# Expert one-hot codes laid out by pairs of tokens, in operations of eight tokens

## The chip, the core and the metric

The kernel runs on one core of a Trainium2 chip. The metric is the device time of one execution in microseconds; the median of three runs is 1916.95 us (1915.26 to 1919.09). TensorE (PE) multiplies, VectorE (DVE), ScalarE (ACT) and GpSimd (POOL) work element by element, and SyncE (SP) issues most transfers.

## What is computed

The whole kernel is a block of three mixers (windowed attention, a gated recurrence, attention over a memory), an expert layer, a delta-rule layer, a dilated-window attention and two plain feed-forward layers, on 256 tokens of width 1024 in float32. The change lies in the expert layer alone:

```python
idx = jnp.take_along_axis(cand_i, best_pos, axis=-1)
gate = jax.nn.softmax(best_v, axis=-1)
u = u_tab[ix]
act = jax.nn.gelu(jnp.einsum('chkd,cd->chk', u, hx).astype(jnp.float32))
vv = v_tab[ix]
return jnp.einsum('chk,chkd->cd', (gx * act).astype(vv.dtype), vv)
```

Each token picks 8 x 16 = 128 experts of 16384 and weighs each with a gate. An expert's index is a pair: a first key (0 to 127) and a second key (0 to 127).

## The kernel before

The kernel doesn't gather. It multiplies each token with all 16384 rows of `peer_u` (128 chunks of 128 experts, `gemm_y`), keeps the activations as `act` (second key on the partitions, first key and token on the free axes), multiplies `act` with a gate that is zero for the experts a token did not pick, and multiplies the result with all 128 chunks of `peer_v` (`gemm_k`). Each chunk is 24 matmuls: weights and operand are each split into a high and a low part of float32r (`whi` by ACT, `wlo` by DVE or POOL), and three of the four products are added. For `peer_u` POOL makes every second `wlo`; for `peer_v` DVE makes all.

The gates of a token form a 128 x 128 matrix (second key by first key). `scatter` (L1071) builds it from one-hot codes. The 128 picks of a token lie on the partitions; `i1T`, `i2T` hold the first and second key of each pick by token, `g2T` the gate as a high and a low half in float16. For four tokens at a time DVE makes `oh2` (L1080, 128 x 128 x 4: does the second key equal the number in `iota4`), `oh1` (L1083, 128 x 64 x 4, half of the first keys) and `ohg` (L1086, `oh1` times both halves of the gate, 128 x 2 x 64 x 4). PE then adds, for each token, `oh2` (weights, 128 columns) times `ohg` (64 columns moving) for both halves of the gate into the token's 64 columns of a PSUM bank `gp`. Eight tokens fill the bank; DVE then multiplies `act` with it in place (L1094).

All codes lie in one tile, `ohp` (4096 float16 per partition), with the token innermost: `oh2` has three places of 512, `oh1` two of 256, `ohg` three of 512. A matmul takes one token, so PE reads every fourth element. A DVE operation that reuses a place waits for the matmuls that read it.

`scatter(half)` runs for 64 of the first keys over the 256 tokens, 32 rounds of eight tokens. It is a generator with two yields a round (after the codes and matmuls, and after the product with `act`). `bg.step` (class `Bg`) takes as many steps after each chunk as the constants say, so that the code's place in the loop sets the order: `scatter(0)` runs beside `peer_u` chunks from 73 on (1.3 steps a chunk, `UP`), `scatter(1)` beside the first 64 `peer_v` chunks (one step a chunk). [...] Two PSUM banks serve `gp` in turn (`aux`).

Of the kernel before, what the change touches and what calls it, by code (L numbers as in the profile page):

```python
# [15 lines left out]
F16 = mybir.dt.float16  # L16
AF = mybir.ActivationFunctionType
ALU = mybir.AluOpType
# [344 lines left out]
def build(tc, a, out, stop=None, dbg=None):  # L363
    nc = tc.nc
    V, S, PE, G = nc.vector, nc.scalar, nc.tensor, nc.gpsimd
    ctx = ExitStack()
    with ctx:
# [65 lines left out]
        def mm(o, l, r, start, stop):  # L433
            x = PE.matmul(o, l, r, start=start, stop=stop, skip_group_check=True)  # L434
            if dbg is not None:
                dbg.append((st.plan[st.nu - 1][0], x.ins.name))
# [13 lines left out]
        def aux(nm="aux"):  # L450
            return aux_p.tile([128, 512], F32, name=nm, tag="aux")
# [170 lines left out]
        with ExitStack() as pa:  # L622
# [35 lines left out]
            for c in range(4):  # L658
                hi, lo = st.get(("w_vm", c))
                for j in range(2):  # L660
                    kt = c * 2 + j
                    w = slice(j * 512, (j + 1) * 512)
                    for t in range(2):
                        tt = slice(t * 128, (t + 1) * 128)
# [154 lines left out]
            for c in range(2):  # L819
                hi, lo = st.get(("w_va", c))  # L820
                for j in range(4):
                    kt = c * 4 + j
                    w = slice(j * 256, (j + 1) * 256)
                    for t in range(2):
                        o = vps[:, t * 256:(t + 1) * 256]
                        tt = slice(t * 128, (t + 1) * 128)
# [63 lines left out]
            for n in range(8):  # L890
                if n + NG < 8:
                    gts.append(gates(n + NG))
                g = gts.pop(0)
# [48 lines left out]
        with ExitStack() as pb:  # L942
            B1 = pb.enter_context(tc.tile_pool(name="B1", bufs=1))
            bp = pb.enter_context(tc.tile_pool(name="bp", bufs=2))
# [10 lines left out]
            for t in range(2):  # L955
                for g in range(4):
                    p = aux("sc")
# [11 lines left out]
            i1T, i2T = i12T[:, 0, :], i12T[:, 1, :]  # L969
            g2T = bp.tile([128, 2, T], F16, name="g2T", tag="g2T", bufs=1)  # L970
# [3 lines left out]
            iota = bp.tile([128, 128], F32, name="iota", bufs=1)  # L974
# [90 lines left out]
                    V.scalar_tensor_tensor(g2T[:, 1, w], gf, GS, g2T[:, 0, w], op0=ALU.mult, op1=ALU.subtract)  # L1065
                    yield

            iota4 = bp.tile([128, 128, 4], F16, name="iota4", tag="iota4", bufs=1)
            V.tensor_copy(iota4, iota[:, :, None].to_broadcast([128, 128, 4]))

            def scatter(half):  # L1071

                c0 = half * 64
                for t0 in range(0, T, 8):
                    p = aux("gp")
                    for k in (0, 4):
                        tt = slice(t0 + k, t0 + k + 4)
                        i = (t0 + k) // 4
                        oh2 = ohp[:, 512 * (i % 3):512 * (i % 3) + 512].rearrange("p (c t) -> p c t", t=4)
                        V.tensor_tensor(oh2, iota4, i2T[:, None, tt].to_broadcast([128, 128, 4]), op=ALU.is_equal)  # L1080
                        o1 = 1536 + 256 * (i % 2)
                        oh1 = ohp[:, o1:o1 + 256].rearrange("p (c t) -> p c t", t=4)
                        V.tensor_tensor(oh1, iota4[:, c0:c0 + 64, :], i1T[:, None, tt].to_broadcast([128, 64, 4]), op=ALU.is_equal)  # L1083
                        o1 = 2048 + 512 * (i % 3)
                        ohg = ohp[:, o1:o1 + 512].rearrange("p (q c t) -> p q c t", q=2, t=4)
                        V.tensor_tensor(ohg, oh1[:, None, :, :].to_broadcast([128, 2, 64, 4]),  # L1086
                                        g2T[:, :, None, tt].to_broadcast([128, 2, 64, 4]), op=ALU.mult)
                        for j in range(4):
                            for q in range(2):
                                mm(p[:, (k + j) * 64:(k + j + 1) * 64], oh2[:, :, j], ohg[:, q, :, j],  # L1090
                                   k == 0 and j == 0 and q == 0, q == 1)
                    yield
                    av = act[:, c0:c0 + 64, t0:t0 + 8]
                    V.tensor_tensor(av, p.rearrange("p (t c) -> p c t", c=64), av, op=ALU.mult)  # L1094
                    yield
# [7 lines left out]
            bg.drain()  # L1103
            ohp = res.tile([128, 4096], F16, name="ohp", tag="x")
            bg.add(scatter(0))
            for c in range(UP[0], 128):
                ps = gemm_y(("peer_u", c), hb)
                S.activation(act[:, c, :], ps, AF.Gelu_apprx_tanh)
                with tc.issue_after(st.lasts[-LAG]):
                    bg.step(UP[2])  # L1110
            bg.drain()
            bg.add(scatter(1))
            acc = acc_new()
            cq = (opr.tile([128, 8, T], F32R, name="chi", tag="xhi"), opr.tile([128, 8, T], F32R, name="clo", tag="xlo"))
# [26 lines left out]
        with ExitStack() as pc:  # L1141
# [413 lines left out]
            for c, h in gorder:  # L1555
# [9 lines left out]
                elif c == "v":  # L1565
                    vf = cp.tile([128, T], F32, name="vf", tag="vf")
                    conv(ps, 16 + h, vf)
                    p = aux("vT")
# [71 lines left out]
        with ExitStack() as pd:  # L1640
# [26 lines left out]
            for j in range(2):  # L1667
                p = aux("trc")
# [16 lines left out]
            for w in (slice(0, 512), slice(512, 768)):  # L1685
                p = aux("bias")
                p = p[:18, :w.stop - w.start]
# [131 lines left out]
        c = N.sums()  # L1819
# [31 lines left out]
```

## Time and profile before

| what | value |
|---|---|
| median of three runs | 1916.95 us (1915.26 to 1919.09) |
| profiled execution, its own time | 1913.9 us |
| its span in the trace | 1912.1 us |
| granted TensorE clock, mean | 0.984 |
| PE / DVE / ACT / POOL busy | 96% / 72% / 51% / 18% |
| DMA | 314.85 MB, 165 GB/s in the mean |

The span runs from the first to the last instruction in the trace; the 1.8 us between span and time lie around it. Busy shares are means over all stages. Matmuls overlap, so what one costs is read from the distance of the starts, or from a run of them on the chain, rather than from its own duration.

### The profile page before, as it was taken

To read this page: it belongs to the slowest core of one execution; us is meant where nothing else is said; L and a number is where in the kernel's file an instruction comes from. 1 tells how busy PE (TensorE), PEld (TensorE's weight loads), DVE (VectorE), ACT (ScalarE), POOL (GpSimd) and SP (SyncE) were. 2 spreads that over 40 slices of the span, in tenths; PEclk is the share of its full clock that TensorE was granted. 3 is DMA by queue.
4 is the path that set the end of the run, shared out by engine and by line. 5 is a ranking of instruction groups with operands and counts; after the bars stand their busy time and mean duration, and the time that the engine had idled before them with its cause. 6 is when DMAs were issued, how large, how long until landed. Compare 5 with 4: busy or idle time off the path is not lost.

```text
span 1912.1 us, 38492 instructions
## 1 busy us (share of the span) xinstructions
PE 1835.9 (96%) x15622; PEld 1799.8 (94%) x15622; DVE 1375.9 (72%) x2644; ACT 974.2 (51%) x1589; POOL 344.7 (18%) x202
## 2 busy tenths in 40 slices
PE   8999999999999999999999998878999999999998
PEld 7989999999999999999999997767999999999998
DVE  8698666887868777888865558996575556766555
ACT  6587444545443334444354455634755456555554
POOL 2010002344443332000000026553130001010000
PEclk9999999999999999999999998889999999999998
DMA  6534566455654445455566664344156666645663
GB/s 229 181 122 140 181 193 209 149 186 177 189 174 155 149 152 165 158 163 156 160 204 188 188 205 132 93 97 115 47 163 188 189 189 205 191 134 187 189 188 109
DMA packets 113704, 314.85 MB, mean 165 GB/s; under 512 B 35043, under 2 KB 38243, under 8 KB 112759
## 3 DMA queue, kind: packets, MB, share of 16 engines
q1 hardware_dynamic: 112390, 305.82, 52.4%
q0 software_dynamic: 1136, 6.59, 1.0%
q8 instruction: 122, 2.00, 0.4%
q14 instruction: 56, 0.45, 0.1%
HBM read 307.06 MB, written 5.30 MB: 163 GB/s over the span
## 4 chain that ended last, share of the span: by engine, by line
PE 82%; DVE 14%; ACT 2%; issue 2%; DMA 0%; POOL 0%; DVEq 0%; SPq 0%; ACTq 0%
PE mmps L434 37%; PE acc L434 34%; PE gp L434 3%; DVE wlo L206 2%; PE p L434 2%; PE vps L434 1%; DVE cy L1265 1%; DVE tk L1042 1%; DVE U L1303 1%; ACT whi L202 1%; DVE tk L1040 1%; DVE kv L1349 1%; DVE eg L1461 1%; DVE mxl L443 1%; PE lg L434 1%
## 5 line engine op out<-in xcount | busy, mean ns | idle before, releaser
L202 ACT ACTIVATE whi<-wraw 128x1024 fp32r<-128x1024 f32 x562 | 595.7, 1061 | 775.1 <-PE acc L434 296.9
L206 DVE TENSOR_TENSOR wlo<-wraw,whi 128x1024 fp32r<-128x1024 f32 x461 | 569.7, 1237 | 306.0 <-ACT whi L202 303.0
L204 POOL TENSOR_TENSOR wlo<-wraw,whi 128x1024 fp32r<-128x1024 f32 x101 | 247.1, 2449 | 672.1 <-ACT whi L202 577.2
L434 PE MATMUL mmps<-bhi,whi 128*128 128x256 f32 x1024 | 288.9, 282 | 1.9 <-ACT act L1100 1.9
L434 PE MATMUL mmps<-bhi,wlo 128*128 128x256 f32 x1024 | 285.8, 279 | 3.1 <-DVE wlo L206 3.1
L434 PE MATMUL mmps<-blo,whi 128*128 128x256 f32 x1024 | 285.8, 279 | 0.0
L434 PE MATMUL acc<-chi,whi 128*128 128x256 f32 x1008 | 283.4, 282 | 0.0
L434 PE MATMUL acc<-clo,whi 128*128 128x256 f32 x1008 | 281.3, 279 | 0.3 <-DVE clo L441 0.3
L434 PE MATMUL acc<-chi,wlo 128*128 128x256 f32 x1008 | 281.1, 279 | 0.0
L434 PEld LDWEIGHTS mmps<-bhi,wlo 128*128 128x128 f32 x1024 | 192.5, 188 | 3.5 <-DVE wlo L206 3.5
L434 PEld LDWEIGHTS mmps<-bhi,whi 128*128 128x128 f32 x1024 | 193.2, 189 | 2.5 <-ACT act L1100 2.5
L434 PEld LDWEIGHTS mmps<-blo,whi 128*128 128x128 f32 x1024 | 192.6, 188 | 0.0
L434 PEld LDWEIGHTS acc<-clo,whi 128*128 128x128 f32 x1008 | 189.5, 188 | 0.5 <-DVE clo L441 0.5
L434 PEld LDWEIGHTS acc<-chi,whi 128*128 128x128 f32 x1008 | 189.9, 189 | 0.0
L434 PEld LDWEIGHTS acc<-chi,wlo 128*128 128x128 f32 x1008 | 189.4, 188 | 0.0
L434 PE MATMUL acc<-rl,whi 128*128 128x256 f32 x512 | 142.8, 279 | 0.0
L434 PE MATMUL acc<-rh,wlo 128*128 128x256 f32 x512 | 142.8, 279 | 0.0
L434 PE MATMUL acc<-rh,whi 128*128 128x256 f32 x512 | 142.4, 279 | 0.0
L434 PE MATMUL mmps<-mxl,whi 128*128 128x256 f32 x496 | 139.3, 281 | 1.4 <-DVE mxl L443 1.0
L434 PE MATMUL mmps<-mxh,wlo 128*128 128x256 f32 x496 | 138.9, 280 | 0.8 <-DVE wlo L206 0.8
L434 PE MATMUL mmps<-mxh,whi 128*128 128x256 f32 x496 | 138.6, 280 | 0.8 <-ACT mxh L439 0.5
L434 PE MATMUL mmps<-xhi,whi 128*128 128x256 f32 x384 | 111.2, 289 | 1.8 <-DVE qm L862 1.3
(578 smaller groups left out, 4429.3 us busy)
## 6 DMA issues: line engine op xcount, KB each, us to landing
wraw<-in_peer_u SPq DMA_DIRECT2D x128, 512.0 KB, 3.6
wraw<-in_peer_v SPq DMA_DIRECT2D x128, 512.0 KB, 3.8
wraw<-in_w SPq DMA_DIRECT2D x128, 512.0 KB, 4.2
wraw<-in_w_gates SPq DMA_DIRECT2D x24, 512.0 KB, 3.6
wraw<-in_p_all SPq DMA_DIRECT2D x16, 512.0 KB, 3.8
wraw<-in_w_peer_q SPq DMA_DIRECT2D x16, 512.0 KB, 3.8
wraw<-in_d_v SPq DMA_DIRECT2D x12, 512.0 KB, 4.4
wraw<-in_d_q SPq DMA_DIRECT2D x9, 512.0 KB, 4.4
```

The lines of the kernel that those rows point to most:

```text
L202: nc.scalar.activation(hi, t, AF.Copy)
L204: nc.gpsimd.tensor_tensor(lo, t, hi.bitcast(F32), op=ALU.subtract)
L206: self.lasts.append(nc.vector.tensor_sub(lo, t, hi.bitcast(F32)).ins)
L434: x = PE.matmul(o, l, r, start=start, stop=stop, skip_group_check=True)
L443: return V.scalar_tensor_tensor(lo, src, scale, hi.bitcast(F32), op0=ALU.mult, op1=ALU.subtract).ins
L1040: V.tensor_tensor(eq, io16, rank[:, s, None].to_broadcast([128, 32, 16]), op=ALU.is_equal)
L1042: V.tensor_tensor(eq.rearrange("p (h k) c -> p h k c", h=2), eq.rearrange("p (h k) c -> p h k c", h=2), tif4[:, h:h + 2, p2, None, :].to_b ...
L1265: V.scalar_tensor_tensor(y[:, lo_:hi_], x[:, lo_ + d:hi_ + d], col("gdn_conv", j * 24 + base), y[:, lo_:hi_], op0=ALU.mult, op1=ALU.add)
L1303: V.scalar_tensor_tensor(U[:, u, :], kk[:, h, t, :], rk2b[:, t, d, h:h + 1], D[:, u, :], op0=ALU.mult, op1=ALU.mult)
L1349: V.tensor_tensor(q, M[:, 0:i, 0:i].rearrange("p j c -> p c j"), L[:, i, None, 0:i].to_broadcast([128, i, i]), op=ALU.mult)
L1461: (G if QE == "G" else V).tensor_mul(qe[d], qe[d], qf[:, h, (1 - d) * 128:(2 - d) * 128])
```

## The change

The codes are made for eight tokens in one operation. The free axes are now four pairs of tokens, key, and token of the pair, so that the two tokens of a pair lie next to each other and PE reads every second element. `iota4` keeps its size, but only its first half (`iota2`, 128 x 2) is filled and read, repeated over the pairs. `oh2` has two places of 1024, `oh1` one of 512, and the gate product is made in two operations, one for each half of the gate, in three places of 512. The matmuls run over the eight tokens for the high half of the gate, then over the eight tokens for the low half; only the very first still starts the bank.

```diff
--- before.py
+++ after.py
@@ -1065,30 +1065,28 @@
                     V.scalar_tensor_tensor(g2T[:, 1, w], gf, GS, g2T[:, 0, w], op0=ALU.mult, op1=ALU.subtract)
                     yield
 
-            iota4 = bp.tile([128, 128, 4], F16, name="iota4", tag="iota4", bufs=1)
-            V.tensor_copy(iota4, iota[:, :, None].to_broadcast([128, 128, 4]))
+            iota4 = bp.tile([128, 2, 128, 2], F16, name="iota4", tag="iota4", bufs=1)
+            iota2 = iota4[:, 0]
+            V.tensor_copy(iota2, iota[:, :, None].to_broadcast([128, 128, 2]))
 
             def scatter(half):
 
                 c0 = half * 64
                 for t0 in range(0, T, 8):
                     p = aux("gp")
-                    for k in (0, 4):
-                        tt = slice(t0 + k, t0 + k + 4)
-                        i = (t0 + k) // 4
-                        oh2 = ohp[:, 512 * (i % 3):512 * (i % 3) + 512].rearrange("p (c t) -> p c t", t=4)
-                        V.tensor_tensor(oh2, iota4, i2T[:, None, tt].to_broadcast([128, 128, 4]), op=ALU.is_equal)
-                        o1 = 1536 + 256 * (i % 2)
-                        oh1 = ohp[:, o1:o1 + 256].rearrange("p (c t) -> p c t", t=4)
-                        V.tensor_tensor(oh1, iota4[:, c0:c0 + 64, :], i1T[:, None, tt].to_broadcast([128, 64, 4]), op=ALU.is_equal)
-                        o1 = 2048 + 512 * (i % 3)
-                        ohg = ohp[:, o1:o1 + 512].rearrange("p (q c t) -> p q c t", q=2, t=4)
-                        V.tensor_tensor(ohg, oh1[:, None, :, :].to_broadcast([128, 2, 64, 4]),
-                                        g2T[:, :, None, tt].to_broadcast([128, 2, 64, 4]), op=ALU.mult)
-                        for j in range(4):
-                            for q in range(2):
-                                mm(p[:, (k + j) * 64:(k + j + 1) * 64], oh2[:, :, j], ohg[:, q, :, j],
-                                   k == 0 and j == 0 and q == 0, q == 1)
+
+                    pairs = lambda x: x[:, t0:t0 + 8].rearrange("p (g t) -> p g t", t=2)[:, :, None, :]
+                    i = t0 // 8
+                    oh2 = ohp[:, 1024 * (i % 2):1024 * (i % 2) + 1024].rearrange("p (g c t) -> p g c t", g=4, t=2)
+                    V.tensor_tensor(oh2, iota2[:, None].to_broadcast([128, 4, 128, 2]), pairs(i2T).to_broadcast([128, 4, 128, 2]), op=ALU.is_equal)
+                    oh1 = ohp[:, 2048:2560].rearrange("p (g c t) -> p g c t", g=4, t=2)
+                    V.tensor_tensor(oh1, iota2[:, None, c0:c0 + 64].to_broadcast([128, 4, 64, 2]), pairs(i1T).to_broadcast([128, 4, 64, 2]), op=ALU.is_equal)
+                    for q in range(2):
+                        o1 = 2560 + 512 * ((2 * i + q) % 3)
+                        ohg = ohp[:, o1:o1 + 512].rearrange("p (g c t) -> p g c t", g=4, t=2)
+                        V.tensor_tensor(ohg, oh1, pairs(g2T[:, q]).to_broadcast([128, 4, 64, 2]), op=ALU.mult)
+                        for j in range(8):
+                            mm(p[:, j * 64:(j + 1) * 64], oh2[:, j // 2, :, j % 2], ohg[:, j // 2, :, j % 2], j == 0 and q == 0, q == 1)
                     yield
                     av = act[:, c0:c0 + 64, t0:t0 + 8]
                     V.tensor_tensor(av, p.rearrange("p (t c) -> p c t", c=64), av, op=ALU.mult)
```

## Rows read from the trace of the kernel before

**Rows 1.** The page: engines, and the granted clock in 40 slices.

```profile
PE 1835.9 (96%) x15622; PEld 1799.8 (94%) x15622; DVE 1375.9 (72%) x2644; ACT 974.2 (51%) x1589; POOL 344.7 (18%) x202
...
PEclk9999999999999999999999998889999999999998
```

**Rows 2.** Windows of both stages: us, busy (instructions), clock, DMA.

```profile
core 0: us, PE busy (x) PEld busy (x) DVE busy (x) ACT busy (x) POOL busy (x), PEclk, DMA share, GB/s
560.00:740.00 180.00, 180.00 (x1768) 178.78 (x1767) 142.65 (x265) 69.27 (x104) 63.19 (x26) 1.00 0.50 155
754.00:962.00 208.00, 207.77 (x1989) 206.63 (x1990) 170.42 (x336) 85.18 (x123) 0.00 (x0) 1.00 0.51 158
```

**Rows 3.** Waits of PE and PEld, 560 to 970: total, times, longest.

```profile
PE acc L434 <- DVE clo L441: 0.3, 1, 0.3
...
PEld acc L434 <- DVE clo L441: 0.5, 1, 0.5
```

**Rows 4.** The chain in the peer_v stage: start us, us, what.

```profile
768.03 1.00 PE gp L434 x16
769.03 5.65 PE acc L434 x48
774.68 1.01 PE gp L434 x16
...
962.03 182.09 PE acc L434 x1560
```

**Rows 5.** Tiles ohp, identb on PE: ns min/median/max, first and last start.

```profile
L434 PEld LDWEIGHTS <-ohp x1024: 111/117/137, 566.3 to 961.7; 128*128 128x128 f16 x171
L434 PE MATMUL gp<-ohp x1024: 219/243/247, 566.3 to 961.8; 128*128 128x64 f16 x171
...
L434 PEld LDWEIGHTS <-identb x16: 95/98/147, 1185.1 to 1210.9; 128*128 128x128 bf16 x16
```

**Rows 6.** DVE operations by tile and by line, same columns.

```profile
L1080 DVE TENSOR_TENSOR ohp<-iota,i12T x128: 407/420/2107, 561.5 to 954.9; 128x512 f16<-128x512 f16 x128
L1083 DVE TENSOR_TENSOR ohp<-iota,i12T x128: 273/283/2289, 562.0 to 951.5; 128x256 f16<-128x256 f16 x128
L1086 DVE TENSOR_TENSOR ohp<-ohp,g2T x128: 408/418/2109, 564.5 to 957.2; 128x512 f16<-128x512 f16 x128
...
L1094 DVE TENSOR_TENSOR act<-gp,act x64: 676/692/694, 568.2 to 962.1; 128x512 f32<-128x512 f32 x64
...
L1040 DVE TENSOR_TENSOR tk<-iota,tk x16: 677/691/2715, 402.7 to 539.5; 128x512 f32<-128x512 f32 x16
...
L1069 DVE CAST iota<-iota x1: 428/428/428, 288.2 to 288.2; 128x512 f16<-128x512 f32 x1
```

**Rows 7.** Waits of DVE, 560 to 740, then 754 to 962.

```profile
DVE ohp L1080 <- PE gp L434: 33.1, 17, 2.9
...
DVE ohp L1080 <- PE gp L434: 22.9, 29, 1.1
```

**Rows 8.** Timeline of one burst: start us, us, what, idle before.

```profile
801.19 1.16 PE L434 MATMUL gp<-ohp 128*128 128x64 f16 x16
...
801.89 0.43 DVE L1080 TENSOR_TENSOR ohp<-iota,i12T 128x512 f16<-128x512 f16 x1 [0.77 <-PE gp L434]
...
802.39 0.69 DVE L1094 TENSOR_TENSOR act<-gp,act 128x512 f32<-128x512 f32 x1
...
802.99 1.22 DVE L206 TENSOR_TENSOR wlo<-wraw,whi 128x1024 fp32r<-128x1024 f32 x1
...
804.13 0.42 DVE L1086 TENSOR_TENSOR ohp<-ohp,g2T 128x512 f16<-128x512 f16 x1
```

**Rows 9.** Timeline, small f32 matmuls of the delta-rule layer.

```profile
1322.66 0.68 PE L434 MATMUL acc<-XY,U 64*64 64x64 f32 x16
```

## The prediction

> **What bounds the kernel now.** I read the page's engine table and slices first, then the two stages in which the changed code runs, then PE's own waits there, the chain, and last the rows of the instructions that change. PE is busy for 96% of the span [rows 1]. `scatter` runs beside the peer_u matmuls (about 560 to 740 us) and beside the peer_v matmuls (about 754 to 962 us). [...] PE and its weight loads together wait 0.8 us for another engine between 560 and 970 us [rows 3]. So in these stages the time is the number of PE's instructions times what each occupies PE, and nothing DVE saves is worth anything by itself. The chain says the same: it alternates between runs of 48 main matmuls (5.65 us) and one burst of 16 `gp` matmuls (1.00 to 1.01 us) [rows 4]. One burst is eight tokens; 32 in each half make 64, or 64.3 us of the span at 1.005 us each. That is the pool this change can touch.
>
> What one `gp` matmul costs: 1.005 us / 16 = 62.8 ns. A main matmul streams 256 columns and the long run at the chain's end puts 1560 in 182.09 us, 116.7 ns each [rows 4]; in proportion, 64 columns are 29.2 ns. So 33.6 ns of each `gp` matmul is not the streaming of its columns. Part of it shows in the weight load: loading 128x128 f16 from `ohp`, with 8 bytes from one element to the next, takes 117 ns in the median, and loading the 128x128 bf16 identity, which lies without gaps, takes 98 ns [rows 5]. Both are two-byte loads of the same shape, so I put the 19 ns down to the gaps.
>
> **The change, part by part.**
>
> PE's reads. There are still 1024 weight loads of 128x128 and 1024 matmuls of 64 columns, but both operands now have 4 bytes from one element to the next instead of 8. No row shows a step of 4 bytes, so its price is bounded. At worst it reads like 8 bytes (117 ns, nothing gained). At best the load is like the one without gaps (98 ns) and saves 19 ns on each of 1024, 19.5 us. If the columns too stream with a penalty now, the farthest bound is the whole remainder of 33.6 ns, 34.4 us. A denser step giving a loss would need a cost that no row hints at; I leave a loss of this part at nothing. Between the ends I count the excess as growing with the gap: a step of 2 bytes has none, 8 bytes has 19 ns, so 4 bytes keeps (4 - 2) / (8 - 2), a third, 6.3 ns, and saves 12.7 ns. That nearness to the row without gaps is why I take more than half. 1024 x 12.7 ns = 13.0 us, straight on the path, since the burst follows the main matmuls without a gap and nothing but PE's own work ends either run [rows 3, 4].
>
> PE's order. The burst now runs gate half 0 for eight tokens, then gate half 1, instead of both halves token by token. The same weights were loaded twice in a row and are still loaded twice (1024 loads for 1024 matmuls [rows 5]), so the order neither saves nor adds a load. Zero; the main matmuls already add into one region three times running at 116.7 ns each, so back-to-back accumulation was not costing anything to be regained.
>
> DVE's operations. Per eight tokens there were two each of the 512-element code (420 ns), the 256-element code (283 ns) and the 512-element gate product (418 ns) [rows 6]: 2242 ns. Now there is one of 1024 elements and three of 512. From 256 to 512 elements the code costs 137 ns more, 0.535 ns an element over a fixed 146 ns, so 1024 elements are 694 ns if pairs keep that rate, and the sum is 694 + 3 x 420 = 1954 ns. 64 times 288 ns is 18.4 us of DVE less, all of it beside PE work: DVE already spends 33.1 and 22.9 us of the two stages waiting for `gp` matmuls to free `ohp` [rows 7]. On the path: zero. The one-time cast of the iota row halves; it stands alone at 288 us with 0.43 us and nobody waits for it [rows 6].
>
> DVE's wait. Before, the wait sits on the 512-element code of a group of four tokens, whose buffer is one of three: the row at 801.89 us starts 0.77 us late, right behind the first half of the burst that began at 801.19 [rows 8]. Afterwards the 1024-element code has two buffers of its own and finds one free, and the gate products share three places, so the wait moves to the second gate product, which reuses the place of the first one of the burst before. It ends at the same event, the eighth matmul of a burst. Queued behind it are the product into `act`, the `wlo` subtraction and `clo`; those stood behind the old wait too, and less code work follows it now. Cost zero, hidden by the main matmuls between two bursts; without that cover it would be the 0.77 us per burst, 24.6 us over the second half's 32.
>
> What is late next if the burst shrinks: a pair of chunks goes from 6.65 to about 6.45 us, DVE's share of it is 82% of 6.65 = 5.45 us less 0.29, so DVE stays at 80% and DMA near 52%. PE keeps the path and the 13.0 us reach the end.
>
> Sum: the profiled execution takes 1913.9 us (span 1912.1 and 1.8 around it), less 13.0 gives 1900.9. The median of the runs is 1916.95, 3.05 above that execution, so on the scale of the runs I predict **1904.0 us**.
>
> **Rivals.**
>
> *Nothing changes.* The excess of the load belongs to any gap between elements, whatever its width, or to a fixed cost of a short burst; pairs then read like fours, and the time stays 1917. For it: the 62.8 ns do not split by any row into load and stream, and only one gapped operand exists in the trace. Against a fixed cost of issue: a run of 16 loads and 16 matmuls of 64x64 f32 takes 0.68 us [rows 9], where a `gp` burst takes 1.16 by the same view [rows 8], so PE can start pairs faster than this. [...] Chance 0.25.
>
> *DVE loses its packed rate and becomes the bound, slower.* The broadcast index operand now repeats two values (one 4-byte word) 128 times, where it repeated four. If DVE then takes elements one at a time, as the f32 comparison of 512 elements does at 691 ns [rows 6], an element costs (691 - 146) / 512 = 1.064 ns: 1236 ns for the code of 1024 elements and 691 for each of the others, 3309 ns against 2242, 1.07 us more per burst. DVE's waits for `gp` are the slack: 33.1 / 32 = 1.03 us per burst in the first stage and 22.9 / 31 = 0.74 in the second (208 us at 6.65 a burst are 31) [rows 7]. The rest, 0.04 and 0.33 us, delays `wlo` and with it PE: 32 x 0.37 = 12 us, 1929 on the runs' scale. It decides once DVE's code work per eight tokens passes 2.24 + 0.74 = 2.98 us. Against it: the f32 comparison itself repeats one 4-byte word 16 times per row, and its fastest, 677 ns, is no slower than the 676 of the product into `act`, which repeats nothing [rows 6]. [...] Chance 0.08, with 0.03 more for small losses from a changed order of instructions.
>
> **How the numbers follow.** PE's reads getting cheaper with the step: 0.64, likeliest near 13 us, from 4 to 24 us for most of it (own range 1893 to 1913). Nothing: 0.25. Slower: 0.11. The runs before spread over 0.2% (1915.26 to 1919.09), so 0.2%, 3.8 us, is about what a measurement can tell from no change; a saving under 3.7 ns per matmul counts as the same. The range runs from 1893 (24 us saved, the load's 19.5 and a little of the stream) to 1920, the top of the unchanged case; it leaves out the slower case and the last of the 34.4 us.
>
> **What would show it.** Right: the `ohp` weight load falls from 117 towards 104 ns, a `gp` burst on the chain from 1.00 to about 0.80 us, the 48 main matmuls stay at 5.65 us, PE still waits for nothing in the two stages, DVE's 1024-element code is near 0.69 us, and its wait stands on the gate product. Load and burst unchanged: the first rival. A 1024-element code over 1.2 us with PE waiting for `wlo`: the second. I am wrong in size if the burst falls but the load doesn't, since then the columns' streaming was what the gaps slowed.

## The result, and the profile after

The changed kernel takes 1885.84 us in the median of four runs (1884.27 to 1886.58), the kernel before 1916.11 beside it (1912.49 to 1919.09): a ratio of 0.9846, 95% interval 0.9832 to 0.9859. That is 30.3 us faster, in the interval 27.0 to 32.2. I forecast 12 to 13 us with a range down to 1893, so the direction was right, the size was wrong by more than a factor of two, and the result lies below the range.

The profiled execution has its span at 1884.8 us, 27.3 below the 1912.1 of before. The chain that ended last, in the peer_v stage (start us, us, what), answers to [rows 4]; the last line is the long run after the last burst:

```profile
764.65 0.50 PE gp L434 x16
765.15 5.69 PE acc L434 x48
770.83 0.50 PE gp L434 x16
771.33 5.73 PE acc L434 x48
```

```profile
932.70 183.86 PE acc L434 x1560
```

A burst of 16 `gp` matmuls went from 1.005 to 0.50 us, 31 ns a matmul in place of 62.8. 64 bursts give 64 x 0.505 = 32.3 us, and that is the whole gain. A little is given back in the runs between the bursts: a run of 48 main matmuls takes 5.69 or 5.73 us where it took 5.65, and the long run 183.86 where it took 182.09. The first is about 0.06 us for some 31 runs in this stage, 1.8 us, the second 1.8 us. The runs beside `peer_u` give back as much each. Two of them before, then two after:

```profile
599.01 5.66 PE mmps L434 x48
605.67 2.85 PE mmps L434 x24
```

```profile
604.06 5.73 PE mmps L434 x48
610.29 2.89 PE mmps L434 x24
```

Over that stage's chain a run is about 0.05 us longer, 1.5 us for 31 runs. Together 5.1 us go back, which accounts for 32.3 - 27.3.

The instructions of `ohp` (duration ns min/median/max, first and last start), against [rows 5, 6]:

```profile
L434 PEld LDWEIGHTS <-ohp x1024: 96/97/101, 565.0 to 932.5; 128*128 128x128 f16 x171
L434 PE MATMUL gp<-ohp x1024: 190/193/205, 565.0 to 932.5; 128*128 128x64 f16 x171
L1087 DVE TENSOR_TENSOR ohp<-ohp,g2T x128: 410/424/2621, 563.9 to 926.3; 128x512 f16<-128x512 f16 x128
L1081 DVE TENSOR_TENSOR ohp<-iota,i12T x64: 674/683/2775, 560.2 to 922.2; 128x1024 f16<-128x1024 f16 x64
L1083 DVE TENSOR_TENSOR ohp<-iota,i12T x64: 407/415/2426, 561.0 to 922.8; 128x512 f16<-128x512 f16 x64
```

Both PE rows fell: the weight load from 117 to 97 ns, the matmul from 243 to 193. DVE's operation of 1024 elements takes 683 ns in the median and that of 512 takes 415, 0.523 ns an element between them; between the 512 and 256 elements of before it was 0.535 [rows 6]. So pairs keep the rate of the fours. The two windows, shortened with their stages, against [rows 2], and the waits of PE and of DVE from 555 to 960 us against [rows 3, 7]:

```profile
560.00:735.00 175.00, 175.00 (x1850) 173.63 (x1849) 149.03 (x199) 73.71 (x112) 68.00 (x27) 1.00 0.54 169
750.00:945.00 195.00, 195.00 (x1997) 193.72 (x1997) 162.32 (x271) 87.09 (x130) 0.56 (x1) 1.00 0.56 176
```

```profile
PE acc L434 <- DVE clo L441: 0.5, 1, 0.5
PE acc L434 <- ACT chi L439: 0.4, 1, 0.4
```

```profile
DVE ohp L1087 <- PE gp L434: 34.0, 44, 2.2
```

PE still fills both windows at the full granted clock (1.00), and its matmuls wait for 0.9 us in all. DVE's wait for the `gp` matmuls now stands on the gate product (L1087), 34.0 us in place of 33.1 and 22.9.

### The profile page after: what moved, and what is told of

Same layout as the page of the kernel before. It is cut to its first block, busy times and chain, and to the rows that moved or that the text cites. A ratio compares the mean times of both kernels' runs of the same rounds, so it can differ in the third digit from the quotient of the medians.

```text
span 1884.8 us, 38363 instructions
## 1 busy us (share of the span) xinstructions
PE 1807.0 (96%) x15622; PEld 1770.4 (94%) x15622; DVE 1372.0 (73%) x2516; ACT 974.5 (52%) x1589; POOL 347.5 (18%) x202
## 4 chain that ended last, share of the span: by engine, by line
PE 81%; DVE 14%; ACT 2%; issue 2%; DMA 0%; POOL 0%; DVEq 0%; SPq 0%; ACTq 0%
PE mmps L434 37%; PE acc L434 35%; DVE wlo L206 3%; PE p L434 2%; PE gp L434 2%; PE vps L434 1%; DVE cy L1263 1%; DVE tk L1042 1%; DVE U L1301 1%; ACT whi L202 1%; DVE tk L1040 1%; DVE kv L1347 1%; DVE eg L1459 1%; DVE mxl L443 1%; PE lg L434 1%
```

## The experiments

Three questions were open. Which of PE's two reads set the 62.8 ns, the weights' or the moving columns'? Did the larger operations or the new order of matmuls have a part? And what is it in the layout that costs, the distance between neighbours or something coarser? The first four kernels are whole ones, with a ratio and its interval each; the seven named s are the changed kernel with only PE's read addresses altered, and there the burst on the chain is the evidence.

**Weights in pairs, moving columns in fours.**

```diff
 # against the changed kernel
-oh1 = ohp[:, 2048:2560].rearrange("p (g c t) -> p g c t", g=4, t=2)
+oh1 = ohp[:, 2048:2560].rearrange("p (g c t) -> p g c t", g=2, t=4)
-    ohg = ohp[:, o1:o1 + 512].rearrange("p (g c t) -> p g c t", g=4, t=2)
+    ohg = ohp[:, o1:o1 + 512].rearrange("p (g c t) -> p g c t", g=2, t=4)
-        mm(..., oh2[:, j // 2, :, j % 2], ohg[:, j // 2, :, j % 2], ...)
+        mm(..., oh2[:, j // 2, :, j % 2], ohg[:, j // 4, :, j % 4], ...)
 # left out: iota4 and the tokens that DVE reads, which follow the layout
```

> Operations of eight tokens as in the change; the weights (second-key codes) in pairs, the moving gate products in fours. Stream theory (the 8-byte step slows the 64 moving columns, and that alone sets the distance of the matmuls): weight load 97 ns, matmul near 243 ns, a burst stays at 0.95 to 1.0 us, time 1913 to 1917. Load theory (the slow weight load set the distance): burst 0.5 to 0.6 us, time near 1887. Both add up: burst near 0.7 us (1.005 less 16 x 20 ns), time near 1897.

Ratio to before 0.9998 (0.9988 to 1.0008): nothing is gained. Chain and `ohp` rows:

```profile
768.10 0.98 PE gp L434 x16
769.08 5.65 PE acc L434 x48
```

```profile
L434 PEld LDWEIGHTS <-ohp x1024: 96/117/118, 566.5 to 961.2; 128*128 128x128 f16 x171
L434 PE MATMUL gp<-ohp x1024: 219/241/244, 566.5 to 961.3; 128*128 128x64 f16 x171
```

The burst stays at 0.98 us. The load's row is the surprise: the weights now lie 4 bytes apart, as in the changed kernel, yet the median load still takes 117 ns, where it took 97 in the changed kernel; only the fastest takes 96. So a load's recorded duration depends on the moving read beside it too, and my 117 against 98, taken where both reads had gaps, could not price the weights' layout.

**Weights in fours, moving columns in pairs.** The mirror image of the edit above: `oh2` with g=2, t=4, its matmuls reading `oh2[:, j // 4, :, j % 4]`, the rest as in the changed kernel.

> The other half: weights in fours, moving gate products in pairs. Stream theory: matmul 193 ns, weight load 117 ns hidden behind the running matmul, burst 0.5 to 0.65 us, time 1886 to 1895. Load theory: burst stays near 1.0 us, time near 1915. Both add up: burst near 0.8 us, time near 1904.

Ratio 0.9888 (0.9871 to 0.9904), 1892.56 us against 1914.49, 21.9 us faster:

```profile
767.65 0.56 PE gp L434 x16
768.21 5.69 PE acc L434 x48
```

```profile
L434 PEld LDWEIGHTS <-ohp x1024: 111/117/132, 566.2 to 937.3; 128*128 128x128 f16 x171
L434 PE MATMUL gp<-ohp x1024: 192/197/221, 566.2 to 937.4; 128*128 128x64 f16 x171
```

The burst is 0.56 us with a load of 117 ns: most of the gain comes from the moving columns alone, 0.445 of the 0.505 us of a burst, and 23.1 of the 27.3 us between the spans (1889.0 us here). The weights' layout is worth the 0.06 us a burst from here to 0.50; beside gapped columns, in the run before, it was worth about 0.02. The row of the load stands at 117 ns again, this time for the weights' own gaps, so it reads the same whichever of the two reads has them.

**Operations of eight tokens, layout still in fours.** `oh2`, `oh1` and `ohg` all with g=2, t=4; buffers, operation sizes and order of matmuls as in the changed kernel.

> Everything of the change (operations of eight tokens, the two gate halves one after the other, its buffers) except the layout: codes and gates stay in fours. Stream and load theory alike: burst 1.0 us, time as before, 1913 to 1917, though DVE is about 18 us less busy. Grouping theory (fewer, larger operations or the new order of matmuls give the gain): burst below 0.8 us, time below 1900.

Ratio 1.0001 (0.9991 to 1.0011), and the burst as before:

```profile
766.39 1.00 PE gp L434 x16
```

**Pairs, operations still of four tokens.**

```diff
 # against the kernel before
-oh2 = ohp[...].rearrange("p (c t) -> p c t", t=4)
+oh2 = ohp[...].rearrange("p (g c t) -> p g c t", g=2, t=2)
-oh1 = ohp[:, o1:o1 + 256].rearrange("p (c t) -> p c t", t=4)
+oh1 = ohp[:, o1:o1 + 256].rearrange("p (g c t) -> p g c t", g=2, t=2)
-V.tensor_tensor(ohg, oh1[:, None, :, :]..., g2T[:, :, None, tt]..., op=ALU.mult)
+for q in range(2):
+    V.tensor_tensor(ohg[:, q], oh1, tok(g2T[:, q])..., op=ALU.mult)
-        mm(..., oh2[:, :, j], ohg[:, q, :, j], ...)
+        mm(..., oh2[:, j // 2, :, j % 2], ohg[:, q, j // 2, :, j % 2], ...)
```

> The layout alone: pairs in the kernel of before, operations of four tokens, both gate halves token by token, its buffers (the gate product becomes two operations of 256, so DVE has 2 x 2 x 283 ns in place of 2 x 418 a burst more). Stream and load theory: burst 0.5 us, time 1884 to 1890, DVE being hidden. Grouping theory: burst 1.0 us, time 1913 to 1920. If DVE's extra 0.3 us a burst matters, a few us over 1886 with PE waiting for a subtraction of the next weights.

Ratio 0.9868 (0.9851 to 0.9884), 1887.99 us against 1914.49; this interval overlaps that of the changed kernel (0.9832 to 0.9859), so no part of the gain is shown to belong to the grouping:

```profile
767.34 0.50 PE gp L434 x16
```

**What in the moving read costs.** Seven kernels differ from the changed one only in what the matmul reads: the moving operand, in the first the weights too, in the fourth the weights alone. (In the last two the output is written in the same runs, to the same places.) All read as many elements as before, but other ones, so the gates are not the reference's. The edits, with `fg` for the 512 elements of a gate product and `f2` for the 1024 of a code:

```diff
 # s1 (2 bytes, weights too)   f2[:, j*128:(j+1)*128], fg[:, j*64:(j+1)*64]
 # s2 (6 bytes)                fg[:, 4*j:4*j+190:3]
 # s3 (16 bytes)               fg[:, j::8]
 # s4 (weights at 16 bytes)    f2[:, j::8], moving pairs
 # s5 (32 bytes)               f2[:, j::16] as the moving operand
 # s6 (runs of 2 every 16 B)   fg[...].rearrange("p (a b) -> p a b", b=8)[:, :, 0:2]
 # s7 (runs of 4 every 16 B)   fg[...].rearrange("p (a b) -> p a b", b=8)[:, :, 0:4]
```

> The changed kernel, but PE reads other elements of the same places: weights and moving columns with 2 bytes from one element to the next (the gates come out wrong, the amount of work is the same). If the 4-byte step already streams at the full rate: matmul 193 ns, burst 0.47 to 0.50 us, time as the changed kernel. If a step costs in proportion to its bytes: burst towards 0.45 us (64 columns at the main matmul's rate), 2 to 3 us less.

> The changed kernel with the moving columns read at a step of 6 bytes (other elements, same count), the weights at 4. Both the theory of 8-byte words (48 words hold 64 columns) and that of cost in proportion to the bytes spanned give 46 to 47 ns a matmul and a burst of 0.75 us. A threshold (slow as soon as neighbours are over 4 bytes apart) gives 62 ns and 1.0 us; a threshold at 8 gives 0.5 us.

> The changed kernel with the moving columns read at a step of 16 bytes, the weights at 4. Words of 8 bytes (one column a word, as at 8 bytes): burst 1.0 us, time near 1914. In proportion to the bytes spanned, or by 16-byte lines (one column a line): 124 ns a matmul, burst 2.0 us, time near 1978, if DVE's codes stay hidden.

> The changed kernel with the weights read at a step of 16 bytes, the moving columns at 4. Stream theory with the load hidden up to some length: at 8 bytes the load took 20 ns more and the burst 0.06 us more (0.56). Words of 8 bytes: as at 8 bytes, 117 ns and 0.56 us. By lines or by bytes spanned: load near 157 ns or more, and the load, no longer hidden, sets the distance: burst 0.9 to 1.2 us.

> The changed kernel with the moving columns read at a step of 32 bytes, out of the place of the second-key codes (the only place long enough; the gate products are made but not read), weights at 4 bytes. Lines of 16 bytes (each new line costs about 1.85 ns, however far away it is): 117 ns a matmul as at 16 bytes, burst near 1.87 us, time near 1966. In proportion to the bytes spanned: about 235 ns a matmul, burst 3.7 us, time near 2080.

> The changed kernel with the moving columns read as 32 runs of two neighbours, a run every 16 bytes, weights at 4 bytes. Lines: 32 lines for 64 columns, as the fours had: 62 ns, burst 1.0 us, time near 1913. If what counts is that neighbours lie together (two in one 4-byte word), whatever the line: 30 ns or the floor, burst 0.5 us, time near 1886.

> The same with 16 runs of four neighbours, a run every 16 bytes. Lines: 16 lines for 64 columns, as the pairs have: 30 ns, burst 0.5 us, time near 1886, though the bytes spanned are those of a 4-byte step only in the mean and the hop between runs is 10 bytes. If every hop costs something of its own: 16 hops, burst 0.6 to 0.75 us.

One burst of each from the chain, in the order s1, s2, s3, s5, s6, s7:

```profile
765.63 0.48 PE gp L434 x16
```

```profile
767.11 0.76 PE gp L434 x16
```

```profile
841.28 1.87 PE gp L434 x16
```

```profile
848.21 1.90 PE gp L434 x16
```

```profile
841.77 0.98 PE gp L434 x16
```

```profile
840.09 0.50 PE gp L434 x16
```

Each ran once: 1890.10, 1901.55, 1965.86, 1917.06, 1974.22, 1914.62 and 1886.25 us from s1 to s7, beside a kernel before of 1913.70 (s1 to s4) or 1911.71 (s5 to s7). Runs of one kernel differ by several us (1912.49 to 1919.09 before), so these times weigh less than the bursts. Two are longer than their bursts say. In s1, 3.0 us more than in the changed kernel lie behind the last burst, where the kernels are the same (955.3 us to the end against 952.3); in s5, PE waits 4.2 us for DVE in the two stages.

Set beside the number of 16-byte lines, stretches of 16 bytes, that 64 columns touch (counted from the addresses):

| moving read | lines | burst us | ns a matmul | ns a line |
|---|---|---|---|---|
| 2 bytes apart | 8 | 0.48 | 30 | |
| 4 bytes apart (the change) | 16 | 0.50 | 31 | |
| runs of 4, every 16 bytes | 16 | 0.50 | 31 | |
| 6 bytes apart | 24 or 25 | 0.76 | 47.5 | 1.94 |
| 8 bytes apart (before) | 32 | 1.005 | 62.8 | 1.96 |
| runs of 2, every 16 bytes | 32 | 0.98 | 61 | 1.91 |
| 16 bytes apart | 64 | 1.87 | 117 | 1.83 |
| 32 bytes apart | 64 | 1.90 | 119 | 1.86 |

From 24 lines up, the time of a matmul is 1.83 to 1.96 ns for each line; below that it rests on a floor of 30 to 31 ns, and whether the columns, the loads or the issue make that floor no run here separates. The theory of 8-byte words falls with s3: at 8 and at 16 bytes every word yields one column, yet 16 bytes cost nearly twice as much (1.87 us a burst against 1.005). Cost by bytes spanned falls with s5, which spans twice the bytes of s3 at nearly the same price (1.90 us against 1.87). That two neighbours lie together is not enough (s6, 0.98 us), and a hop of 10 bytes between runs of four costs nothing (s7, 0.50 us). In the table the time follows how many columns each line yields: four or more run at the floor (30 to 31 ns), two take twice the time (61 to 62.8), one takes nearly four times (117 to 119). That the line is a fixed one is not shown: no run moves a group of columns across a boundary, so a cost that grows with the mean distance of neighbours and stops growing near 16 bytes would give the same table.

The weights' layout has a cost of its own, much smaller at 8 bytes (0.06 us a burst) than the columns' (0.48 with the weights in pairs); at 16 bytes it stands on the chain (rows of s4, chain and `ohp`):

```profile
769.18 1.01 PE gp L434 x16
```

```profile
L434 PEld LDWEIGHTS <-ohp x1024: 142/171/176, 565.4 to 964.2; 128*128 128x128 f16 x171
L434 PE MATMUL gp<-ohp x1024: 224/224/254, 565.4 to 964.3; 128*128 128x64 f16 x171
```

At 16 bytes apart, 128 weights touch 128 lines, and with the weights' addresses alone changed the distance rises from 31 to 63 ns a matmul. That is 0.49 ns a line, about a quarter of the 1.83 to 1.96 ns that a line of the moving read takes.

## Why the prediction was right in direction and wrong in size

**What bounds the kernel: right.** PE's own instructions set the time of both stages before and after, and what a burst lost came off the time, but for the few us given back in the main runs.

**PE's reads: this is the step that failed.** I split the 62.8 ns of a matmul into 29.2 ns of streaming and a remainder, looked for the remainder in the weight load, found 19 ns there and took two thirds of them. Both moves were wrong. In the trace of before the 16 loads of the burst at 801.18 us take 0.98 us beside its 16 matmuls, which take 1.16 [rows 8]:

```profile
801.18 0.98 PEld L434 LDWEIGHTS <-ohp 128*128 128x128 f16 x16
```

Repairing the weights alone changes nothing (0.9998), repairing the columns alone takes 21.9 us off. So the load's excess was hidden. That the load sets the distance only when it is the longer of the two is my reading of bursts of 0.98 us (weights in pairs, columns in fours), 0.56 (fours, pairs) and 1.01 (weights at 16 bytes, columns in pairs); no run times the two apart. And the streaming of 64 columns was not 29.2 ns, a proportion taken from a main matmul whose 256 columns of four bytes lie without gaps, four to a line; 64 columns 8 bytes apart lie on 32 lines, two to a line, and take 62.8. The term should have been 1024 x (62.8 - 31) = 32.6 us. It is close to the far bound I had worked out (33.6 ns, 34.4 us) and had then left out of the range, though no row spoke against it. One even pointed there: 16 loads and 16 matmuls of 64 columns took 0.68 us [rows 9], of another shape and type, and the changed burst takes 0.66 by the same view:

```profile
801.73 0.66 PE L434 MATMUL gp<-ohp 128*128 128x64 f16 x16
```

I had used that row against a fixed cost of issue only.

The interpolation failed too: the cost of the moving read does not grow evenly with the step from 2 bytes on. It is flat from eight columns a line to four (0.48 and 0.50 us a burst) and then about in proportion to the lines (0.76 us at 24 or 25 lines, 1.005 at 32, 1.87 at 64).

**My test for it would have misled me.** I wrote that a burst that falls while the load doesn't would point to the streaming. The load's row fell as well, to 97 ns, and would have seemed to confirm the load. The first two experiments show that the row stands at 117 ns as soon as either read goes by 8 bytes, so it could not have told them apart.

**The order of matmuls at zero: right,** as the fours in operations of eight show (1.0001).

**DVE: right on the path, wrong in sum.** The large operation takes 683 ns where I said 694, and the wait moved to the gate product, as told. But of 18.4 us less DVE work only 3.9 are seen (1375.9 to 1372.0 us busy). In the peer_u stage DVE's share even rose from 79 to 85%: its operations are stretched there while POOL makes every second `wlo`, and now the largest one is hit. In both traces every code operation of that stage that took over one and a half times its median lies beside a POOL `wlo`, 17 before and 25 after; beside `peer_v`, where POOL makes none, no operation is stretched so. By line (busy, mean ns, idle before), first before from 560 to 740 us, then after from 560 to 735:

```profile
L1086 DVE TENSOR_TENSOR ohp<-ohp,g2T 128x512 f16<-128x512 f16 x67 | 53.0, 792 | 0.1
```

```profile
L1081 DVE TENSOR_TENSOR ohp<-iota,i12T 128x1024 f16<-128x1024 f16 x34 | 48.9, 1439 | 0.0
...
L1083 DVE TENSOR_TENSOR ohp<-iota,i12T 128x512 f16<-128x512 f16 x34 | 16.0, 472 | 0.0
```

The mean of 792 ns stood beside a median of 418, that of 1439 stands beside 683. PE still waited for only 0.9 us in all, so it cost next to nothing here.

**The rivals.** "Nothing changes" held that pairs read like fours. They do not: two float16 columns a line take 0.98 to 1.005 us a burst, four take 0.50. The other rival, DVE falling to the 1.064 ns an element that I worked out from the f32 comparison, would have needed over 1.2 us for the large operation. 683 ns excludes it, though its operand repeats one 4-byte word where the fours repeated two.

## What to carry to other kernels

When a short matmul costs more than its columns in proportion, count the 16-byte lines that its moving operand touches before blaming the weight load: here a float16 operand needed four of its elements in every line (0.50 us a burst, with two 0.98 to 1.005), and no more than that (0.48 with eight). A duration in a row of an engine that overlaps two streams belongs to neither of them alone (the load's row read 117 ns with either operand in fours), so the split is made by changing one stream at a time. And a bound that no row speaks against belongs into the range.

## What had not been expected of the hardware

Besides the cost by lines: the main matmuls, untouched by the change, run in one of two steady paces. After the last burst 1560 of them took 182.09 us before (116.7 ns each) and 183.86 after (117.9 ns each). The seven other kernels with a burst of 0.76 us or more had 182.04 to 182.18, those with 0.56 or less (the changed kernel, gates in pairs, pairs by four, 2 bytes, runs of four) all 183.86. Between the bursts of the changed kernel both paces stand in turn: in the run that began at 789.97 us the second matmul starts at 790.01 and the last at 795.38, 46 steps of 116.7 ns, and in the next from 796.19 to 801.61, 46 steps of 117.8; on the chain these are the runs of 5.69 and 5.73 us. So the pace can change at a burst, and the one behind the last burst stays. Why, none of these runs tells; behind the last burst it is 1.8 us of 1885.
